# Retention in chunks of 64 on quarters of the array, with the rotation taken straight out of the banks

## The chip, the core and the metric

The kernel runs on one core of a Trainium2 chip. Its engines are TensorE (PE, matrix products; PEld is its weight load), VectorE (DVE), ScalarE (ACT), GpSimd (POOL) and SyncE (SP), which only issues transfers. Each works through its own queue in order and waits on semaphores for the others. Products land in eight banks of PSUM (128 partitions of 512 fp32 values); all other data lies in SBUF. The metric is the device time of one execution in microseconds; three runs of the kernel before took 1176.33, 1178.77 and 1178.81, median 1178.77.

## The reference

A trunk of two layers on 1024 tokens of width 1024, fp32. Layer 0 normalises the input, projects it, and runs two branches: an S5 state-space layer with a GLU, and retention with 8 heads (keys and queries of 64, values of 128). Layer 1 is a Conformer convolution module. The change is in the retention, chunk by chunk of 64 tokens:

```python
scores = jnp.einsum('bnihd,bnjhd->bnhij', qc, kc) * intra
intra_out = jnp.einsum('bnhij,bnjhe->bnihe', scores, vc)
kv = jnp.einsum('bnjhd,jh,bnjhe->bnhde', kc, k_dec, vc)
def state_step(s, kv_n):
    return chunk_decay * s + kv_n, s
cross = jnp.einsum('bnihd,ih,bnhde->bnihe', qc, q_dec, s_prev)
out = (intra_out + cross)          # then normalised per head and token
```

Queries and keys are rotated first (rope: x1 cos - x2 sin, x1 sin + x2 cos on the two halves of 32). The outcome is multiplied by a gate and goes into the output projection.

## The kernel before

The large projections run on TensorE as three fp32r products with a weight split into high and low parts (`mm3`, L276 to L278), 24 products of 512 columns for one half (512 tokens) of a 128-row tile. After layer 0's front (to 345 us) come the values (to 435), then four head pairs one after another, then the GLU and layer 1.

For one pair, `ret_proj` (L974) projects keys and queries of two heads onto 128 partitions. VectorE multiplies the bank by the token's norm factor `R` (L987), four DMAs on SyncE swap halves of 32 rows (L996), GpSimd multiplies the plain and the swapped copy by cosine and sine (L1000, L1002; two halves of 512 each), VectorE adds them (L1003). `ret_heads` (L1079) then works in blocks of 128 tokens, each two chunks with a mask that hides the second chunk from the first: it transposes the keys (L1088) and weights them with the decay (kt, L1090); makes the key-value product of each block (kv, L1107); sums the state S on VectorE (L1115, L1117), one block after another, each step needing the one before; makes the scores (sp, L1124) and masks them (sc, L1130); adds the cross product with S (L1154) and the intra product with the values (L1159) in one bank (ro) per head and half; takes mean and variance (L1168, L1169), a reciprocal root on ScalarE and VectorE (rs), and normalises (on, L1174); transposes back (rt, L1182) and multiplies by the gate (grl, L1185). Products that use half of the rows or columns of the array are written alternately so that two can run at once.

The banks are taken in turn from a small ring, so a new product can wait until an older bank was read. Pairs 0 to 2 project the keys (and then the queries) of the next pair ahead, and TensorE has these products between the retention steps. Weight lows (`weight_low`, tiles lf and lh: load, cast on ScalarE, subtraction on GpSimd or VectorE, store) for layer 1 run beside it, 18 of them by pair 2. The queues are not written out by hand: a scheduler orders the instructions of each engine by its own costs, and `issue_after` only keeps one engine's order.

## Time and profile before

| | us |
|---|---|
| median of 3 runs | 1178.77 |
| profiled execution: span of the core | 1173.9 |
| TensorE busy | 1161.3 (99%) |
| VectorE busy | 910.5 (78%) |
| GpSimd busy | 713.5 (61%) |
| ScalarE busy | 545.1 (46%) |

The span runs from the first to the last instruction; the time of a run has 4.9 us more around it. The granted clock is 0.999. In the row of a timeline stand start, length, engine, line, output and inputs, the tile of the array, shapes and a count; a bracket gives idle time and what ended it. Lengths of neighbouring products overlap, so their cost is read from one start to the next.

### The profile page before, as it was taken

To read this page: it belongs to the slowest core of one execution; us is meant where nothing else is said; L and a number is where in the kernel's file an instruction comes from. 1 tells how busy PE (TensorE), PEld (TensorE's weight loads), DVE (VectorE), ACT (ScalarE), POOL (GpSimd) and SP (SyncE) were. 2 spreads that over 40 slices of the span, in tenths; PEclk is the share of its full clock that TensorE was granted. 3 is DMA by queue.
4 is the path that set the end of the run, shared out by engine and by line. 5 is a ranking of instruction groups with operands and counts; after the bars stand their busy time and mean duration, and the time that the engine had idled before them with its cause. 6 is when DMAs were issued, how large, how long until landed. Compare 5 with 4: busy or idle time off the path is not lost.

```text
span 1173.9 us, 17492 instructions
## 1 busy us (share of the span) xinstructions
PE 1161.3 (99%) x6150; PEld 965.5 (82%) x6150; DVE 910.5 (78%) x1507; ACT 545.1 (46%) x821; POOL 713.5 (61%) x507
## 2 busy tenths in 40 slices
PE   9999999999999999999999999999999999999997
PEld 7888888888888888887788888888888888888887
DVE  7875789999717475689777888479999999999643
ACT  7212343332226642123645544367756678544662
POOL 2049999888843245664444034348894689977742
PEclk9999999999999999999999999999999999999999
DMA  9353378778789765765988468965448553357863
GB/s 344 109 178 109 134 270 312 272 269 282 273 307 325 268 228 192 251 190 180 362 313 304 160 220 268 309 232 188 161 158 306 216 182 132 134 176 243 281 247 138
DMA packets 131192, 270.66 MB, mean 231 GB/s; under 512 B 12832, under 2 KB 41760, under 8 KB 130976
## 3 DMA queue, kind: packets, MB, share of 16 engines
q1 hardware_dynamic: 129952, 265.35, 66.5%
q10 hardware_dynamic: 1152, 4.19, 0.9%
q8 instruction: 48, 0.79, 0.3%
q14 instruction: 40, 0.33, 0.1%
HBM read 193.54 MB, written 71.76 MB: 226 GB/s over the span
## 4 chain that ended last, share of the span: by engine, by line
PE 91%; DMA 4%; DVE 2%; SPq 1%; ACT 1%; POOL 1%; issue 1%; DVEq 0%; POOLq 0%; ACTq 0%
PE mm_g L277 8%; PE mm_g L278 8%; PE mm_g L276 7%; PE mm_w L278 4%; PE mm_w L277 4%; PE mm_w L276 4%; PE mm_a L278 2%; PE mm_b L277 2%; PE mm_a L276 2%; PE mm_b L278 2%; PE mm_a L277 2%; PE mm_b L276 2%; PE mm_u L278 2%; PE mm_oc L278 2%; PE mm_u L277 2%; PE mm_oc L277 2%
## 5 line engine op out<-in xcount | busy, mean ns | idle before, releaser
L1461 DVE SCALAR_TENSOR_TENSOR cv<-u,convw,cv 128x512 f32<-128x512 f32 x358 | 244.7, 750 | 5.0 <-ACT cv L1447 3.5
L1441 POOL TENSOR_TENSOR tp<-tp,tp 128x512 f32<-128x512 f32 x104 | 138.9, 1338 | 28.7 <-ACT tp L1440 23.4
L278 PE MATMUL mm_g<-xh,wl_g 128*128 128x512 f32 x256 | 100.8, 394 | 0.0
L277 PE MATMUL mm_g<-xl,wh_g 128*128 128x512 f32 x256 | 100.7, 394 | 0.0
L276 PE MATMUL mm_g<-xh,wh_g 128*128 128x512 f32 x256 | 100.5, 393 | 0.0
L1440 ACT ACTIVATE tp<-u,convw 128x512 f32<-128x512 f32 x104 | 69.6, 713 | 9.6 <-POOL tp L1441 9.4
L277 PEld LDWEIGHTS mm_g<-xl,wh_g 128*128 128x128 f32 x256 | 48.1, 188 | 11.2 <-issue 1.6
L278 PEld LDWEIGHTS mm_g<-xh,wl_g 128*128 128x128 f32 x256 | 48.0, 188 | 10.5
L276 PEld LDWEIGHTS mm_g<-xh,wh_g 128*128 128x128 f32 x256 | 48.1, 188 | 9.6
L278 PE MATMUL mm_oc<-zh,wl_woc 128*128 128x512 f32 (+1 forms) x152 | 54.5, 360 | 0.2 <-DMA wl_woc<-lo_woc 0.2
L276 PE MATMUL mm_oc<-zh,wh_woc 128*128 128x512 f32 (+1 forms) x152 | 54.3, 362 | 0.0
L277 PE MATMUL mm_oc<-zl,wh_woc 128*128 128x512 f32 (+1 forms) x152 | 54.0, 357 | 0.0
L276 PE MATMUL mm_glu<-yh,wh_glu 128*128 128x512 f32 x128 | 50.0, 392 | 1.3 <-ACT sg L1250 1.3
L277 PE MATMUL mm_u<-xl,wh_u 128*128 128x512 f32 x128 | 50.1, 391 | 1.0 <-DVE xl L390 0.9
L276 PE MATMUL mm_g<-h1h,wh_cg 128*128 128x512 f32 x128 | 50.3, 393 | 0.0
L276 PE MATMUL mm_a<-h1h,wh_ca 128*128 128x512 f32 x128 | 50.3, 393 | 0.0
L278 PE MATMUL mm_b<-h1h,wl_cb 128*128 128x512 f32 x128 | 50.3, 393 | 0.0
L232 ACT CAST lh<-lf 128x512 fp32r<-128x512 f32 x32 | 19.5, 618 | 65.9 <-DMA lf<-w_c 59.3
L278 PE MATMUL mm_a<-h1h,wl_ca 128*128 128x512 f32 x128 | 50.0, 391 | 0.0
L277 PE MATMUL mm_glu<-yl,wh_glu 128*128 128x512 f32 x128 | 50.0, 392 | 0.0
L278 PE MATMUL mm_g<-h1h,wl_cg 128*128 128x512 f32 x128 | 49.9, 390 | 0.0
L277 PE MATMUL mm_g<-h1l,wh_cg 128*128 128x512 f32 x128 | 49.9, 390 | 0.0
(811 smaller groups left out, 3637.3 us busy)
## 6 DMA issues: line engine op xcount, KB each, us to landing
wf_g<-w_ab SPq DMA_DIRECT2D x16, 512.0 KB, 5.4
a<-w_out SPq DMA_DIRECT2D x32, 256.0 KB, 4.4
ws<-a SPq DMA_DIRECT2D x32, 256.0 KB, 4.8
lf<-w_c SPq DMA_DIRECT2D x32, 256.0 KB, 5.3
wf_p<-ws SPq DMA_DIRECT2D x16, 512.0 KB, 4.1
wf_cb<-w_c SPq DMA_DIRECT2D x16, 512.0 KB, 4.9
wf_ca<-w_c SPq DMA_DIRECT2D x16, 512.0 KB, 4.7
wl_cb<-lo_cb SPq DMA_DIRECT2D x16, 512.0 KB, 3.4
```

What stands on the lines that cost most here:

```text
L232: self.nc.scalar.copy(hi[:], f[:])
L276: nc.tensor.matmul(ps, wh[:, kb, :], xh, start=start, stop=False)
L277: nc.tensor.matmul(ps, wh[:, kb, :], xl, start=False, stop=False)
L278: self.last_mm = nc.tensor.matmul(ps, wl[:, kb, :], xh, start=False, stop=stop)
L1440: nc.scalar.mul(sk[:], u[:, k:k + HALF], cw[:, nb, k:k + 1])
L1441: gp.tensor_tensor(s0[:], s0[:], sk[:], op=ALU.add)
L1461: v.scalar_tensor_tensor(dst[:], *tap, accs_[i][:], op0=ALU.mult, op1=ALU.add)
```

## The change

The retention works in chunks of 64. Each chunk's decayed keys and values make one product (15 instead of 7 states a pair), with a chunk's token half as rows and a head as columns of a quarter of the array; even and odd chunks go to two banks. Scores are 64 x 64 for each chunk and head, both heads in one bank (partitions 0 to 63 and 64 to 127), so the mask is one VectorE operation for half of the tokens instead of two. Cross and intra products are quarters too. Where a chunk's token half and the head's half differ, the intra product needs the values on the other 64 partitions: four DMAs a pair make the copy `vx` (`crossed`).

The next pair's queries are projected (`fill()`) ahead of the transposes back, and the last of the four quarters of a pair is normalised behind the first transposes. The rotation table is multiplied by `R` once, on GpSimd. Each bank of keys or queries is then read twice by VectorE (sine part, cosine part), the sine part is swapped by the four DMAs, and one addition per half on GpSimd finishes the rotation. The weight lows have three buffers instead of two and come in two groups a pair; the gate tile `grl` has two instead of three.

```diff
+        for i in range(2):
+            for c in (slice(0, HALF), slice(HALF, T)):
+                nc.gpsimd.tensor_tensor(self.rk[:, i, c], self.rk[:, i, c], self.R[:, c], op=ALU.mult)
...
-                last = nc.vector.tensor_tensor(raw[:, c], ps[:], self.R[:, c], op=ALU.mult)
+                for i in (1, 0):
+                    nc.vector.tensor_tensor(parts[nm][i][:, c], ps[:], self.rk[:, i, c], op=ALU.mult)
...
-                nc.sync.dma_start(swp[32 * b:32 * b + 32, :], raw[32 * s:32 * s + 32, :])
-            for c in cs:
-                nc.gpsimd.tensor_tensor(o[:, c], raw[:, c], tab[:, 0, c], op=ALU.mult)
-            for c in cs:
-                nc.gpsimd.tensor_tensor(swp[:, c], swp[:, c], tab[:, 1, c], op=ALU.mult)
-            return o, [lambda c=c: nc.vector.tensor_tensor(o[:, c], o[:, c], swp[:, c], op=ALU.add) for c in cs]
+                nc.sync.dma_start(swp[32 * b:32 * b + 32, :], sin[32 * s:32 * s + 32, :])
+            for c in (slice(0, HALF), slice(HALF, T)):
+                nc.gpsimd.tensor_tensor(o[:, c], cos[:, c], swp[:, c], op=ALU.add)
...
+        def value(p, c, hh, own=False):
+            d, h, b, i = p // 2, c // 8, c // 2 % 4, p % 2
+            if own and c % 2 != hh:
+                return self.vx[:, c // 2, :]
+            return vt[d][h][:, b, (2 * i + hh) * P:(2 * i + hh + 1) * P]
...
+    def crossed(self, pair):
+        d, i = pair // 2, pair % 2
+        self.vx = self.rp.tile([P, 8, P], F32, name=f"vx{pair}", tag="vx", bufs=1)
+        for h in range(2):
+            for hh in range(2):
+                to, of = slice(64 * hh, 64 * hh + 64), slice(64 - 64 * hh, 128 - 64 * hh)
+                self.nc.sync.dma_start(self.vx[to, 4 * h:4 * h + 4, :],
+                                       self.vt[d][h][of, :, (2 * i + hh) * P:(2 * i + hh + 1) * P])
...
-                    nc.tensor.matmul(ps[r, b4 * P:(b4 + 1) * P], kt[:, b, r], V(pair, b, hh),
-                                     start=True, stop=True)
+            self.chained(nc.tensor.matmul(kvs[c % 2][half(hh), col(c)], kt[half(c % 2), c // 2, half(hh)],
+                                          V(pair, c, hh)[half(c % 2)], start=True, stop=True)
+                         for c in cs for hh in range(2))
...
+            sps = self.bank(f"sp{hf}_{pair}")[:].rearrange("p (c i) -> p c i", c=8)
+            self.chained(nc.tensor.matmul(sps[half(hh), c % 8, :], K[half(hh), tok(c)], Q[half(hh), tok(c)],
                                           start=True, stop=True)
+                         for c in range(8 * hf, 8 * hf + 8) for hh in range(2))
...
+                out = lambda c, hh: pss[hh][half(c % 2), c // 2 % 4 * P:(c // 2 % 4 + 1) * P]
+                            yield nc.tensor.matmul(out(c, hh), Q[half(hh), tok(c)], S[half(hh), c - 1, :],
+                                                   start=c in (2, 1, 8, 9), stop=False)
+                        yield nc.tensor.matmul(out(c, hh), sc[half(hh), c, :], V(pair, c, hh, True)[half(hh)],
+                                               start=False, stop=c % 8 > 5)
...
+        on00, on01, on10 = (normed(*a) for a in todo[:3])
+        nxt = fill()
+        last_ro = turn(0, 1, on01, last_ro)
+        last_ro = turn(0, 0, on00, last_ro)
+        on11 = normed(*todo[3])
+        last_ro = turn(1, 0, on10, last_ro)
+        turn(1, 1, on11, last_ro)
```

How it moves instructions, at three places. First, VectorE in pair 0, from the key banks to the second mask, before:

```order
L987 TENSOR_TENSOR kraw_4259<-mm_k_0_4260,R_367 128x512
L987 TENSOR_TENSOR kraw_4259<-mm_k_1_4286,R_367 128x512
L1115 COPY S_4325<-kv_0_4326 128x128
L1117 SCALAR_TENSOR_TENSOR S_4325<-S_4325,g_3507,kv_0_4326 128x128 x3
L1117 SCALAR_TENSOR_TENSOR S_4325<-S_4325,g_3507,kv_0_4339 128x128 x2
L1130 TENSOR_TENSOR sc_0_4349<-sp_0_4351,retmask 128x512
```

and now (kv_0_4336 and kv_0_4337 hold the even and odd chunks of the first half, kv_0_4362 and kv_0_4363 those of the second):

```order
L996 TENSOR_TENSOR ksin_4247<-mm_k_1_4275,ropek 128x512
L996 TENSOR_TENSOR kcos_4246<-mm_k_1_4275,ropek 128x512
L1119 COPY S_4335<-kv_0_4336 128x128
L1121 SCALAR_TENSOR_TENSOR S_4335<-S_4335,g_3511,kv_0_4337 128x128
L1121 SCALAR_TENSOR_TENSOR S_4335<-S_4335,g_3511,kv_0_4336 128x128
...
L1121 SCALAR_TENSOR_TENSOR S_4335<-S_4335,g_3511,kv_0_4362 128x128
L1132 TENSOR_TENSOR sc_4385<-sp_0_4386,retmask 128x512
L1121 SCALAR_TENSOR_TENSOR S_4335<-S_4335,g_3511,kv_0_4363 128x128
...
L1132 TENSOR_TENSOR sc_4385<-sp_0_4404,retmask 128x512
```

The last key bank is read twice instead of once ahead of the copy; the first mask follows the ninth state and the second the fifteenth. On TensorE 11 products of the next queries stand between the two halves of the scores, where 9 stood before.

Second, VectorE in pair 3 from kt to the masks. Before (yl are splits of the GLU's input, sg a step of the GLU):

```order
L1090 TENSOR_TENSOR kt_5352<-ktp_3_5359,kdec 128x512
L1003 TENSOR_TENSOR qrot_5343<-qrot_5343,qswp_5342 128x512 x2
L1194 TENSOR_TENSOR yl_1_5620<-yf_1_5617,yh_1_5619 128x512
...
L1115 COPY S_5372<-kv_3_5373 128x128
...
L1130 TENSOR_TENSOR sc_3_5396<-sp_3_5398,retmask 128x512
L1117 SCALAR_TENSOR_TENSOR S_5372<-S_5372,g_3507,kv_3_5373 128x128
L1130 TENSOR_TENSOR sc_3_5397<-sp_3_5399,retmask 128x512
```

and now:

```order
L1101 TENSOR_TENSOR kt_5577<-ktp_3_5584,kdec 128x512
L1204 TENSOR_TENSOR yl_1_5912<-yf_1_5909,yh_1_5911 128x512
...
L1119 COPY S_5595<-kv_3_5596 128x128
L1204 TENSOR_TENSOR yl_1_5939<-yf_1_5931,yh_1_5938 128x512
L233 TENSOR_TENSOR lh_6079<-lf_6078,lh_6079 128x512
L233 TENSOR_TENSOR lh_6085<-lf_6084,lh_6085 128x512
L1121 SCALAR_TENSOR_TENSOR S_5595<-S_5595,g_3511,kv_3_5597 128x128
L1121 SCALAR_TENSOR_TENSOR S_5595<-S_5595,g_3511,kv_3_5596 128x128
```

Five splits stand between kt and the copy (three before), and one split and two weight lows between the copy and the first step; two more splits stand among the last steps. On TensorE 17 GLU products stand between the two halves of this pair's scores.

Third, TensorE behind the retention products of pair 0, now:

```order
L276 MATMUL mm_q_1_4602<-xh_1_218,wh_q_4171 128x512
L277 MATMUL mm_q_1_4602<-xl_1_219,wh_q_4171 128x512
L278 MATMUL mm_q_1_4602<-xh_1_218,wl_q_4172 128x512
L1183 MATMUL rt_1_4637<-ident,on_0_4549 128x128 x4
L1183 MATMUL rt_0_4643<-ident,on_0_4544 128x128 x4
L1183 MATMUL rt_0_4654<-ident,on_1_4554 128x128 x4
L276 MATMUL mm_k_0_4700<-xh_0_134,wh_k_4241 128x512
```

All 48 products of the next queries now come before the first transpose, 37 of them behind the retention products; 12 of the 48 came behind the first two transposes before. The last quarter's transpose (rt_1) follows 28 products of the next keys later.

More of the change, by code (lines that the diff above doesn't have):

```diff
@@ L951, in retention @@
         nc.sync.dma_start(self.reps[:], A["ret_eps"])
-        ahead = None
+        cur = list(self.ret_proj(0))[-1]
         for pair in range(4):
-            cur = list(ahead or self.ret_proj(pair))[-1]
             if pair == 0:
@@ L958, in retention, with lows @@
                 self.rp = self.pool("ret", 1, stack=st)
+                self.crossed(0)
                 ry = self.pool("retl", 1, stack=early, side="right")
-            with ExitStack() as held:
-                held.enter_context(self.tc.issue_after((self.last_rs if pair else self.last_sum).ins))
-                for k in range(LOWS * pair // 3, LOWS * (pair + 1) // 3) if pair < 3 else ():
-                    self.weight_low(ry, k, (("la", "lb"), ("la", "lb")), 2, nc.gpsimd)
+            def lows(n, behind):
+                with self.tc.issue_after(behind.ins):
+                    for k in range(n * LOWS // 6, (n + 1) * LOWS // 6) if pair < 3 else ():
+                        self.weight_low(ry, k, (("la", "lb"), ("la", "lb")), 3, nc.gpsimd)
             def turned():
+                lows(2 * pair + 1, self.last_kt)
                 if pair == 3:
@@ L968, in turned @@
                     self.lp = self.pool("l1", side="right")
+            lows(2 * pair, self.last_rs if pair else self.last_sum)
             ahead = pair in AHEAD and self.ret_proj(pair + 1)
@@ L971, in retention @@
                 next(ahead)
-            self.ret_heads(pair, *cur, V, turned)
+            cur = self.ret_heads(pair, *cur, V, turned, lambda: list(ahead)[-1] if ahead else None)
+            if pair < 3:
+                self.crossed(pair + 1)
     def ret_proj(self, pair):
         nc, A, rp = self.nc, self.A, self.r0
-        raws = {}
+        parts = {}
         def project(nm):
@@ L980, in project @@
             w = None if early else self.wnext(f"{nm}{pair}")
-            raw = raws[nm] = self.rq.tile([P, T], F32, name=f"{nm}raw_{pair}", tag="raw", bufs=2)
+            parts[nm] = tuple(self.rq.tile([P, T], F32, name=f"{nm}{part}_{pair}", tag=part, bufs=2) for part in ("cos", "sin"))
             for h in range(2):
@@ L995, in turn @@
                 s = b ^ 1
-                nc.sync.dma_start(swp[32 * b:32 * b + 32, :], raw[32 * s:32 * s + 32, :])
-            cs = [slice(h * HALF, (h + 1) * HALF) for h in range(2)]
-            for c in cs:
-                nc.gpsimd.tensor_tensor(o[:, c], raw[:, c], tab[:, 0, c], op=ALU.mult)
-            for c in cs:
-                nc.gpsimd.tensor_tensor(swp[:, c], swp[:, c], tab[:, 1, c], op=ALU.mult)
-            return o, [lambda c=c: nc.vector.tensor_tensor(o[:, c], o[:, c], swp[:, c], op=ALU.add) for c in cs]
+                nc.sync.dma_start(swp[32 * b:32 * b + 32, :], sin[32 * s:32 * s + 32, :])
+            for c in (slice(0, HALF), slice(HALF, T)):
+                nc.gpsimd.tensor_tensor(o[:, c], cos[:, c], swp[:, c], op=ALU.add)
+            return o
         project("k")
         yield None
-        krot, adds = turn("k")
-        last = project("q")
-        with self.tc.issue_after(last.ins):
-            for add in adds:
-                add()
-        qrot, qadds = turn("q")
-        if pair % 2 == 0:
-            for add in qadds:
-                add()
-            qadds = ()
-        yield krot, qrot, qadds
+        krot = turn("k")
+        project("q")
+        yield krot, turn("q")
     def ret_values(self, vp):
@@ L1122, in ret_heads @@
         for hf in range(2):
-            sps = [self.bank(f"sp{hf}{hh}_{pair}") for hh in range(2)]
-            self.chained(nc.tensor.matmul(sps[hh][:, b4 * P:(b4 + 1) * P],
-                                          K[64 * hh:64 * hh + 64, (4 * hf + b4) * P:(4 * hf + b4 + 1) * P],
-                                          Q[64 * hh:64 * hh + 64, (4 * hf + b4) * P:(4 * hf + b4 + 1) * P],
+            sps = self.bank(f"sp{hf}_{pair}")[:].rearrange("p (c i) -> p c i", c=8)
+            tok = lambda c: slice(c * 64, (c + 1) * 64)
@@ L1135, in ret_heads @@
+            self.masked[hf] = v.tensor_tensor(sc[:, 8 * hf:8 * hf + 8, :], sps,
+                                              self.mask[:, pair, :].unsqueeze(1).broadcast_to([P, 8, 64]), op=ALU.mult)
         if pair == 2:
```

128 lines of the change are left out of this document (55 added, 73 removed).

## The prediction

> **What bounds the kernel now.** I read the page's busy table first, then the chain that ended last, then the stretches of the retention stage, then the rows of TensorE there.
>
> ```profile
> PE 1161.3 (99%) x6150; PEld 965.5 (82%) x6150; DVE 910.5 (78%) x1507; ACT 545.1 (46%) x821; POOL 713.5 (61%) x507
> PE 91%; DMA 4%; DVE 2%; SPq 1%; ACT 1%; POOL 1%; issue 1%; DVEq 0%; POOLq 0%; ACTq 0%
> core 0: us, PE busy (x) PEld busy (x) DVE busy (x) ACT busy (x) POOL busy (x), PEclk, DMA share, GB/s
> 435.40:478.40 43.00, 42.73 (x277) 35.84 (x276) 24.77 (x79) 11.28 (x18) 26.10 (x18) 1.00 0.62 207
> 478.40:513.00 34.60, 34.60 (x241) 29.30 (x240) 28.21 (x76) 5.60 (x11) 24.85 (x18) 1.00 0.72 219
> 513.00:552.00 39.00, 37.96 (x255) 31.66 (x254) 32.39 (x84) 14.25 (x25) 21.28 (x14) 1.00 0.64 197
> 552.00:600.00 48.00, 45.99 (x293) 38.64 (x292) 38.48 (x97) 22.46 (x30) 19.41 (x12) 1.00 0.91 336
> 600.00:780.00 180.00, 180.00 (x802) 149.03 (x801) 130.05 (x165) 85.91 (x127) 56.95 (x39) 1.00 0.75 254
> ```
>
> TensorE sets the end: it is busy 99% of the span at full clock, and the chain of waits is 91% its own. In the four rows of the retention stage (one per head pair, roughly) it idles 0.27, 0, 1.04 and 2.01 us, while VectorE works 58 to 83% of the time and GpSimd 40 to 72%. From 600 to 780 it never idles. So a microsecond of TensorE work taken out of the retention stage should come off the end, unless a new wait replaces it. Work taken off GpSimd buys nothing by itself: nothing on the chain waits for it here.
>
> **The retention products.** The rows of TensorE around pair 0 (start, us, line, count) show what the change rewrites. An fp32 product appears as two records.
>
> ```profile
> 447.17 0.39 PE L278 MATMUL mm_k<-xh,wl_k 128*128 128x512 f32 x1
> 447.49 1.75 PE L1107 MATMUL kv<-v,kt 128*64 128x128 f32 x28
> 449.17 1.38 PE L1124 MATMUL sp<-qrot,krot 64*128 64x128 f32 x18
> 450.48 0.51 PE L276 MATMUL mm_q<-xh,wh_q 128*128 128x512 f32 x1
> 450.82 0.40 PE L277 MATMUL mm_q<-xl,wh_q 128*128 128x512 f32 x1
> ...
> 452.46 0.39 PE L278 MATMUL mm_q<-xh,wl_q 128*128 128x512 f32 x1
> 452.77 1.04 PE L1124 MATMUL sp<-qrot,krot 64*128 64x128 f32 x13
> ...
> 454.53 2.05 PE L1159 MATMUL ro<-v,sc 128*128 128x128 f32 x16
> 456.51 1.16 PE L1154 MATMUL ro<-S,qrot 64*128 64x128 f32 x16
> 457.60 2.05 PE L1159 MATMUL ro<-v,sc 128*128 128x128 f32 x16
> 459.41 0.48 PE L276 MATMUL mm_q<-xh,wh_q 128*128 128x512 f32 x1
> ```
>
> From 447.49 to 459.41 are 11.92 us, of which the nine query products in the middle take 450.48 to 452.77, 2.29. Retention proper costs 9.63 us a pair. A record of the intra product, which fills the array, costs 124 ns (16 from 454.53 to 456.51); one that fills half of it costs 60 ns in the key-value product (28 from 447.49 to 449.17), because two of them run side by side.
>
> The change cuts chunks of 128 into 64. The number of records per pair goes from 28+32+28+32=120 to 60+64+60+64=248 (15 chunks with a state and 16 with scores, two heads, two records each), each on a quarter of the array. What does a quarter cost? No row shows one. The nearest above is the half at 60 ns. The nearest below is the S5 kernel's product on four tiles of 32 columns:
>
> ```profile
> 108.80 0.45 PE L882 MATMUL kp<-Mr,s_s_cbr 128*32 128x128 f32 x8
> 109.04 0.42 PE L883 MATMUL kp<-Mi,s_s_cbi 128*32 128x128 f32 x8
> ```
>
> Eight records start within 0.24 us, 30 ns each: four tiles do run together. Row halves pair up (L1124, L1154) and column halves pair up (L1107), and the order of the new products cycles through quarters, so I take 30 ns. The scores use only two of the four quarters at a time (rows and columns of the same head) but stream 64 columns instead of 128: half the length at half the company, 30 ns again. So 248 x 0.030 = 7.4 us. Each handover between these products and the dense ones costs about 0.1 (the usual pitch is (452.46-450.82)/7 = 0.23, and 447.17 plus 0.23 is 447.40, but kv starts at 447.49; the first query product holds 0.34); four of them make 0.4. That is 7.8 against 9.63: **1.8 us saved a pair**. Bounds: at 27 ns 2.5, at 60 ns a loss of 5.6. Break-even is (9.63-0.4)/248 = 37 ns.
>
> **What may wait instead: the state chain.** The state is summed on VectorE one chunk after another, now 15 steps instead of 7.
>
> ```profile
> 447.60 0.69 DVE L987 TENSOR_TENSOR kraw<-mm_k,R 128x512 f32<-128x512 f32 x1 [4.75 <-PE mm_k L278]
> 448.63 0.29 DVE L1115 COPY S<-kv 128x128 f32<-128x128 f32 x1 [0.34 <-PE kv L1107]
> 448.96 1.95 DVE L1117 SCALAR_TENSOR_TENSOR S<-S,g,kv 128x128 f32<-128x128 f32 x5
> 450.82 0.68 DVE L1130 TENSOR_TENSOR sc<-sp,retmask 128x512 f32<-128x512 f32 x1
> 451.43 0.34 DVE L1117 SCALAR_TENSOR_TENSOR S<-S,g,kv 128x128 f32<-128x128 f32 x1
> ```
>
> A step takes 0.37 (five from 448.96 to 450.82), a mask 0.61. In front of the chain now stand two evacuations of the key bank (sine and cosine part) instead of one: 447.60+2x0.67 = 448.95, so the copy starts about 0.3 later. Then copy 0.33, eight steps 2.98, first mask 0.61 (ends 452.9), six steps 2.23 (455.1), second mask (455.7). TensorE: kv 447.5 to 449.3, first scores to 450.3, eleven query products (2.5, plus handovers) to 453.0, second scores to 454.0, first half of ro to 455.8, cross of the second half to 456.8, its intra to 457.7. What it waits for is there in time: the bank of the second ro (freed by the first mask) 1.1 us early, the last state 0.7, the second mask 1.1. So pairs 0 to 2 pay nothing, with a cover of about 0.7 us; in pairs 1 and 2 the first half of the next queries is evacuated at the same place, with the same two operations. If the cover is gone, every 0.1 us on a step costs about 1.4 us a pair, less the cover.
>
> Pair 3 is different: the listing of VectorE has five GLU splits (yl) between kt and the copy, then a sixth and two weight lows (lh), all in front of the chain, and two more inside it.
>
> ```profile
> 553.95 1.75 PE L1107 MATMUL kv<-v,kt 128*64 128x128 f32 x28 [0.67 <-DVE kt L1090]
> 554.41 1.28 DVE L1003 TENSOR_TENSOR qrot<-qrot,qswp 128x512 f32<-128x512 f32 x2
> 555.61 1.89 DVE L1194 TENSOR_TENSOR yl<-yf,yh 128x512 fp32r<-128x512 f32 x3
> 557.41 0.29 DVE L1115 COPY S<-kv 128x128 f32<-128x128 f32 x1
> 556.93 0.50 PE L277 MATMUL mm_glu<-yl,wh_glu 128*128 128x512 f32 x1
> 563.73 1.04 PE L1124 MATMUL sp<-qrot,krot 64*128 64x128 f32 x13
> 568.56 2.05 PE L1159 MATMUL ro<-v,sc 128*128 128x128 f32 x16
> ```
>
> At 0.6 a split: kt 0.6 more, splits 3.1, copy 0.3, split and two lows 1.9, seven steps 2.6, mask 0.6, seven steps and two splits 3.8: the last state is there 12.9 us after kv started. TensorE has kv, two score halves, 17 GLU products (3.9) and half of ro, about 10, before it needs that; the second cross and intra then end near 14.7. Before, the same block ended at 568.56+1.81 = 570.4, 16.4 after kv's start, with more GLU products in it: 556.93 to 563.73 are 6.8 us, 29 or 30 of them. The 12 or so that now come behind the block are 2.8 us. So pair 3 gets 14.7+2.8-16.4 = **1.1 us slower**, instead of 1.8 faster. Bounds: 1.8 gained if the lows come late enough not to matter, 3 lost if the first low waits for its load.
>
> **Next queries in front of the transposes.** The idle time of TensorE that this can take away (total, times, longest):
>
> ```profile
> PE rt L1182 <- DVE on L1174: 1.0, 1, 1.0
> ```
>
> 37 products (8.4 us) now cover the normalisation of the first three quarters in pair 0; I count **1.0** gained, the bounds being 0 and this. The fourth quarter is normalised after 28 further products or, later, after 4; VectorE's rows put it about 1.3 ahead.
>
> **Rotation.** Removed: GpSimd's products (four of eight operations a pair) and VectorE's additions; added: two VectorE products a bank instead of one, and once four products of the table on GpSimd. All of it costs nothing while TensorE's projections cover it, 48 products of 0.23 (11 us) between a projection and its use. At the start the cover is thin:
>
> ```profile
> 355.33 2.53 POOL L1000 TENSOR_TENSOR krot<-kraw,ropek 128x512 f32<-128x512 f32 x2 [18.34 <-DMA ropek<-rope_k]
> 353.29 0.39 PE L1062 MATMUL mm_v<-wh_V,xh 128*128 128x512 f32 x1
> ```
>
> The table lands at 355.3, four products of 1.27 make it ready at 359.1 (first sine half) to 360.4, and the first key bank is free at 360.5. The second half of the queries needs that bank; it now comes after 49 value products, 353.3 + 49 x 0.23 = 364.6. About 4 us to spare; a table that lands 5 us later would cost 1. The swaps on SyncE:
>
> ```profile
> 475.51 2.80 SPq L996 DMA_DIRECT2D qswp<-qraw  x4
> 483.52 3.91 DVE L1003 TENSOR_TENSOR qrot<-qrot,qswp 128x512 f32<-128x512 f32 x2
> 489.18 1.38 PE L1124 MATMUL sp<-qrot,krot 64*128 64x128 f32 x18
> ```
>
> The queries of pair 1 were swapped from 475.5, added up at 483.52+3.91 = 487.4 and used at 489.2. Their swap still queues on SyncE behind weight-low stores, and on GpSimd behind twelve casts of 1.3 instead of ten, but the third buffer lets the loads go earlier and the last step is two additions of 1.27 on GpSimd. I count nothing; without that cover each microsecond that the swap is late is one of TensorE's. Four DMAs a pair copy crossed values on SyncE; they need only the values, which are done before pair 0.
>
> **Sum.** Pairs 0 to 2: -5.4; pair 3: +1.1; transposes: -1.0; total -5.3. The profiled execution had 1173.9 of span, 4.9 under the median of 1178.77 (1176.33 to 1178.81); 1168.6 + 4.9 = **1173.5**.
>
> **Rivals.**
> *Quarters only pair up* (the slower side): 60 ns as for halves. 248 x 0.060 + 0.4 = 15.3, +5.6 a pair, +22 in all, 1200. It decides from 37 ns on. For it: no row has both row and column tiles. Against: the kp rows. 0.10.
> *The chain is late everywhere*: steps of 0.5 rather than 0.37 (held up by other work on VectorE's memory), 14 x 0.13 = 1.8 us a pair, less the cover of 0.7 in three of them: +5.1 in all, 1178.6, no change. For it: one and the same addition of L1003 lasts 1.95 us at 483.52 and 0.64 at 554.41. Against: the steps themselves never varied by more than 12 ns (shortest, median, longest below). 0.17.
>
> ```profile
> L1117 DVE SCALAR_TENSOR_TENSOR S<-S,g,kv x24: 336/347/348, 449.0 to 565.4; 128x128 f32<-128x128 f32 x24
> ```
>
> *Two heads' scores take turns at one bank*: both heads now write one bank, where each had its own. 64 x 0.030 more, 1.9 a pair, 7.7 in all, less the 1.1 of pair 3, which it would cover: 1180, no change. 0.08. [...] No run so far shows it.
> *The turned queries of pair 1 come late*: SyncE's queue holds the swap behind a store whose cast waits for its load. From the additions' end to the use are 1.8 us, and two additions of 1.27 in place of 2.53+3.91 leave about 4 more; beyond 6 us late each microsecond counts. Held by 15 us, sp waits 9: 1182.5. For it: the swap of 475.51 already stood behind such stores. Against: the third buffer. 0.07.
> *All covers hold, pair 3 too, at 27 ns*: 1167. 0.08.
> The forecast keeps 0.50. A measurement here tells no change from 0.2%, 2.4 us. Faster is the forecast, the last rival and a little of the second, 0.60; within 0.2% most of the second and of the third, 0.20; slower the first, the fourth and the rest of those two, 0.20. The range reaches from the best case to the late queries: 1167 to 1183.
>
> **What would show it.** Right: ro records starting 27 to 32 ns apart; no TensorE wait for S or sc in pairs 0 to 2; a wait of 1 to 3 us for S in pair 3; the start of pair 1's kv about 2 us earlier than 487.5. Wrong: records 50 ns apart, a wait of sp for qrot or of mm_q for kcos, or scores at twice the cost of the cross product.

## The result and the profile after

The changed kernel took **1187.03 us** (median of 4 runs, 1186.53 to 1189.67) against 1177.87 (4 runs, 1176.33 to 1178.81) for the kernel before: ratio 1.0078, 95% interval 1.0064 to 1.0092, **9.2 us slower**. The forecast was 1173.5 with a range to 1183.

The two profiles lie 14.0 us apart (spans of 1187.9 and 1173.9). In the recorded runs of the kernel before a time is 1.7 to 1.9 us longer than its span, not 4.9 (that figure sets the median against the span of one faster execution); by that before's execution was an estimated 2.2 under its median, and after's was its slowest run, 2.6 over. So the stages below show where time goes, and some five microseconds of their differences belong to this pair of executions. The first fence is the stretches of the kernel before, the second those of the changed kernel, cut at the first product of each stage: the values, the four pairs with the GLU, the output product, the convolution. Columns: the stretch, its length, then busy time of each engine with its count, and the granted clock after the engines.

```profile
353.30:435.60 82.30, 82.30 (x361) 67.60 (x360) 51.56 (x58) 50.09 (x55) 25.73 (x14) 1.00 0.80 268
435.60:643.30 207.70, 204.39 (x1250) 171.19 (x1249) 154.80 (x376) 74.82 (x117) 111.85 (x70) 1.00 0.76 258
643.30:765.90 122.60, 122.60 (x548) 101.49 (x547) 92.24 (x113) 56.74 (x83) 35.34 (x27) 1.00 0.73 243
765.90:1132.90 367.00, 366.63 (x1637) 301.83 (x1636) 327.91 (x492) 231.44 (x348) 280.10 (x205) 1.00 0.58 197
```

```profile
353.70:440.60 86.90, 84.03 (x362) 68.70 (x361) 50.87 (x58) 50.16 (x55) 26.85 (x14) 0.98 0.77 255
440.60:650.40 209.80, 199.46 (x1762) 166.36 (x1761) 151.46 (x398) 69.63 (x111) 89.54 (x57) 0.98 0.82 263
650.40:777.00 126.60, 123.47 (x549) 101.21 (x548) 92.95 (x116) 59.11 (x87) 36.93 (x27) 1.00 0.70 229
777.00:1147.00 370.00, 366.93 (x1638) 301.82 (x1636) 327.77 (x492) 231.72 (x348) 280.13 (x205) 1.00 0.59 199
```

Read the second row of each. TensorE's busy time in the pairs fell from 204.39 to 199.46 us, as intended. But its idle time there (length less busy) rose from 3.3 to 10.3, so the stretch grew by 2.1. The value stage grew by 4.6, the output product by 4.0 and the convolution by 3.0, though the change does not touch their arithmetic. What TensorE waited for, from the waits of the changed kernel (total, times, longest), and behind them the longest of the kernel before:

```profile
PE mm_glu L276 <- ACT sg L1260: 4.1, 2, 2.8
PE mm_v L1058 <- DVE v L1036: 2.9, 1, 2.9
PE rt L1183 <- DVE mv L1168: 2.8, 1, 2.8
PE mm_w L278 <- DVE wl_p L167: 2.2, 2, 1.4
PE sp L1129 <- DVE S L1121: 2.0, 1, 2.0
PE mm_a L278 <- DMA wl_ca<-lo_ca: 1.6, 1, 1.6
```

```profile
PE mm_glu L276 <- ACT sg L1250: 1.3, 1, 1.3
```

**The clock.** The granted clock is the share of its full clock that TensorE is given. About five of the 9.2 us are lost by work at half clock. In the stretches above the granted clock never fell in the kernel before. In the changed kernel it fell to half three times, for 3.41 us each: once in the value stage behind the wait for v, and twice in the pairs, behind the waits for mv and for S. TensorE's rows, each time the 3.41 us ahead of a fall and then the fall (busy time behind the length, then the granted clock):

```profile
392.02:395.43 3.41, 0.65 (x3) 1.00 1.02 383
395.43:398.84 3.41, 3.41 (x10) 0.50 0.82 282
542.20:545.61 3.41, 1.06 (x8) 1.00 0.69 165
545.62:549.03 3.41, 2.95 (x7) 0.50 0.67 148
562.68:566.09 3.41, 1.45 (x42) 1.00 1.06 407
566.10:569.51 3.41, 3.41 (x65) 0.50 1.06 408
```

At a granted clock of 0.50, with dense products 0.43 us apart instead of 0.23 (value stage), I count half of the busy time in such a stretch as lost: 1.7 us in the value stage, where it makes up the 4.6 together with the wait of 2.9, and (2.95 + 3.41) / 2 = 3.2 us in the pairs. So I estimate TensorE's work in the pairs at full clock at 199.46 - 3.2 = 196.3 us: the change saved 8.1 us there, and 7.0 us more of idle time and 3.2 us of half clock turned that into a loss of 2.1. It is not this one execution: the clocks of the four runs are 0.994 to 0.995, and 1 less the clock, times the span, is 6.8 us in their mean; in the 102 runs of the kernel before that stand beside the experiments it is 1.8.

**The retention products themselves are what was hoped for.** TensorE in pair 0 of the changed kernel:

```profile
452.40 1.86 PE L1113 MATMUL kv<-v,kt 64*64 64x128 f32 x58
454.20 1.09 PE L1129 MATMUL sp<-qrot,krot 64*64 64x64 f32 x30
455.22 0.50 PE L276 MATMUL mm_q<-xh,wh_q 128*128 128x512 f32 x1
...
457.94 0.97 PE L1129 MATMUL sp<-qrot,krot 64*64 64x64 f32 x26
458.92 0.86 PE L1154 MATMUL ro<-S,qrot 64*64 64x128 f32 x23
...
462.52 0.50 PE L278 MATMUL mm_q<-xh,wl_q 128*128 128x512 f32 x1
```

A group's time runs from its first start to its last end, so with 0.27 for one record of ro the 23 start (0.86 - 0.27) / 22 = 27 ns apart, kv's 58 28 ns, and the scores, at 0.22 for one, 30 ns. Retention takes 455.22 - 452.40 plus 462.52 - 457.94, 7.4 us against 9.63. There is no wait in it.

**The value stage.** SyncE's queue before (first fence) and after (second): a row of several transfers lasts until the last of them could be issued.

```profile
356.69 1.07 SPq L1029 DMA_DIRECT2D xf<-xt  x2
357.80 1.06 SPq L931 DMA_DIRECT2D yp<-y_d  x2
359.68 4.32 SPq L1029 DMA_DIRECT2D xf<-xt  x4
```

```profile
350.20 2.55 SPq L1025 DMA_DIRECT2D xf<-xt  x4
352.85 14.82 SPq L931 DMA_DIRECT2D yp<-y_d  x4
...
371.69 0.99 SPq L1025 DMA_DIRECT2D xf<-xt  x1
375.35 0.37 SPq L931 DMA_DIRECT2D yp<-y_d  x1
375.85 2.07 SPq L1025 DMA_DIRECT2D xf<-xt  x2
```

Four loads of the pass over y now stand in a row. They have two buffers (bufs=2), so the third waits until ScalarE has used the first, and the queue stands for 14.8 us. The second group of value loads (xf) is issued from 371.7 and not from 359.7, one by one and again with yp between them. The values' splits, the evacuation v and TensorE follow late (TensorE's rows):

```profile
394.78 0.47 PE L1058 MATMUL mm_v<-wh_V,xth 128*128 128x512 f32 x1 [2.87 <-DVE v L1036]
395.64 0.63 PE L1058 MATMUL mm_v<-wh_V,xth 128*128 128x512 f32 x1
396.07 0.63 PE L1059 MATMUL mm_v<-wl_V,xth 128*128 128x512 f32 x1
```

Not all of this delay comes from yp: in run 5, which takes yp off this queue, the group still begins at 371.7. There it goes out in a row, and ScalarE casts the last of it (xth) at 381.68 instead of 386.75. The late beginning may come from the table (argued, not tested): VectorE's first product out of the banks waits for it until 359.98, where VectorE began at 352.81 before, and the first cast of xf comes at 369.3 instead of 357.6.

**Pairs 2 and 3.** VectorE's rows, first of the kernel before in pair 2, then of the changed kernel in pair 2 and in pair 3:

```profile
529.55 5.74 DVE L1194 TENSOR_TENSOR yl<-yf,yh 128x512 fp32r<-128x512 f32 x4
```

```profile
530.10 0.68 DVE L1132 TENSOR_TENSOR sc<-sp,retmask 128x512 f32<-128x512 f32 x1
530.70 5.87 DVE L1204 TENSOR_TENSOR yl<-yf,yh 128x512 fp32r<-128x512 f32 x6
536.50 1.67 DVE L1167 BATCH_NORM_STATS2 st<-ro 128x6 f32<-128x128 f32 x8
...
556.53 4.16 DVE L1204 TENSOR_TENSOR yl<-yf,yh 128x512 fp32r<-128x512 f32 x5
560.62 0.28 DVE L1119 COPY S<-kv 128x128 f32<-128x128 f32 x1
560.82 0.68 DVE L1204 TENSOR_TENSOR yl<-yf,yh 128x512 fp32r<-128x512 f32 x1
561.42 1.28 DVE L233 TENSOR_TENSOR lh<-lf,lh 128x512 fp32r<-128x512 f32 x2
562.63 2.63 DVE L1121 SCALAR_TENSOR_TENSOR S<-S,g,kv 128x128 f32<-128x128 f32 x7
```

In pair 2 six low halves of the GLU's input (yl) take 5.87 us between the second mask and the statistics; the transposes wait 2.8 for the statistics (mv). The low halves are not new there: before, four of them took 5.74 at the same place. Counted from the start of the pair's kv (522.08 before, 522.61 now), the statistics begin at 13.9 us instead of 13.1, and the transposes even at 21.9 instead of 22.8. But TensorE is done with all that stands ahead of the transposes at 19.1 instead of 21.7: the quarters save 2.2, and two fewer products the rest. So what was saved there became a wait for VectorE. In pair 3 six low halves and two weight lows (lh) stand in front of the chain, and the scores wait 2.0 for S. Behind them the GLU waits 2.8 for a gate (sg) on ScalarE's queue, where the cast of a weight low had waited 5.2 for its load.

### The profile page after: what moved, and what is told of

The parts are those of the page before. It is cut to its first block, busy times and chain, and to the rows that moved or that the text cites. A ratio compares the mean times of both kernels' runs of the same rounds, so it can differ in the third digit from the quotient of the medians.

```text
span 1187.9 us, 18547 instructions
## 1 busy us (share of the span) xinstructions
PE 1159.5 (98%) x6662; PEld 962.4 (81%) x6662; DVE 906.0 (76%) x1531; ACT 542.8 (46%) x819; POOL 693.9 (58%) x495
## 4 chain that ended last, share of the span: by engine, by line
PE 82%; DMA 9%; DVE 4%; ACT 1%; POOL 1%; issue 1%; SPq 1%; DVEq 0%; POOLq 0%; ACTq 0%
PE mm_g L277 7%; PE mm_g L278 7%; PE mm_g L276 7%; PE mm_w L278 3%; PE mm_w L276 3%; PE mm_w L277 3%; PE mm_a L278 2%; PE mm_b L277 2%; PE mm_a L277 2%; PE mm_a L276 2%; PE mm_b L278 2%; PE mm_oc L278 2%; PE mm_u L278 2%; PE mm_b L276 2%; PE mm_u L277 2%; PE mm_oc L277 2%
## 5 line engine op out<-in xcount | busy, mean ns | idle before, releaser
L278 PE MATMUL mm_glu<-yh,wl_glu 128*128 128x512 f32 x128 | 50.5, 394 | 0.0
```

Of the source, the lines that this page charges most:

```text
L278: self.last_mm = nc.tensor.matmul(ps, wl[:, kb, :], xh, start=False, stop=stop)
```

## The experiments

The theories in the expectations. **A**: the quarters save what was planned, and the losses come from queues that the change set in another order (in the value stage above all). **B**: the state chain, twice as long, overloads VectorE. **C**: the queries in front of the transposes do harm. Later ones are defined in the expectations where they first appear. All ratios are to the kernel before, measured beside each run (medians of 1176.9 to 1178.4), with their 95% interval; times of different runs are compared by these ratios; a diff is against the changed kernel unless it says otherwise.

**1. The chunks alone.** The changed kernel with the rotation of before (one product out of the bank, table products on GpSimd, additions on VectorE):

```diff
-                for i in (1, 0):
-                    nc.vector.tensor_tensor(parts[nm][i][:, c], ps[:], self.rk[:, i, c], op=ALU.mult)
+                last = nc.vector.tensor_tensor(raw[:, c], ps[:], self.R[:, c], op=ALU.mult)
...
+        with self.tc.issue_after(self.last_kt.ins):
+            for add in qadds:
+                add()
```

> The changed kernel with the old rotation (raw product, swap, two GpSimd products and one VectorE addition per half); chunks of 64, next queries ahead of the transposes, three buffers of weight lows kept. Theory A (the quarters save 2.2 to 2.7 us a pair as planned, and the loss comes from queues that were put in another order around it, the first of them, 4.6 us in the value stage, by the new rotation): keys of pair 0 transposed at 435 to 437 instead of 440.5, pairs 0 and 1 each 2 us or more shorter than before, total 1176 to 1183. Theory B (the chunks themselves cost the time, since VectorE's longer state chain pushes everything behind it): the value stage may be in time, but the total stays at 1184 to 1188.

Measured 1191.1 us, ratio 1.0118 (1.0101 to 1.0136). The value stage is in time again (82.7 us), which A predicted, but the pairs with the GLU take 223.7 us in place of 209.8, which it did not: TensorE's waits there are headed by

```profile
PE rt L1195 <- DVE on L1189: 7.3, 1, 7.3
PE ro L1166 <- DVE S L1133: 4.8, 1, 4.8
PE rt L1195 <- DVE mv L1180: 4.0, 1, 4.0
```

The time lies outside both ranges. The waits are of B's kind: VectorE's queue is late for S and for the normalisation. That the rotation's additions on it make it late is argued and not shown; in pair 3 VectorE itself stood 2.95 us for GpSimd (yg) and 1.39 for ScalarE (yh) between the steps of the chain. With the chunks, the rotation out of the banks is worth nearly 5 us (1.0118 against 1.0078).

**2. The rotation alone.** The kernel before with the new rotation (diff against it, the reverse of the one above):

```diff
-                last = nc.vector.tensor_tensor(raw[:, c], ps[:], self.R[:, c], op=ALU.mult)
+                for i in (1, 0):
+                    nc.vector.tensor_tensor(parts[nm][i][:, c], ps[:], self.rk[:, i, c], op=ALU.mult)
```

> The kernel before with the new rotation alone (table times R on GpSimd, two VectorE products a bank, one GpSimd addition per half); chunks of 128 and all else as before. Theory A: the value stage loses about 4.6 us, the pairs stay as they were, total 1179 to 1184. Theory B: no loss in the value stage or one made up later, total 1176 to 1179.

Measured 1182.1, ratio 1.0046 (1.0030 to 1.0063). SyncE's queue shows the same row (four yp from 353.2 on, 14.7 us), the wait for v 4.0, the value stage 88.8 us against 82.3, and the pairs 207.0, no worse than before. A holds for the value stage: the loss comes with the rotation, without any chunk of 64.

**3. The next queries at their old place**, behind the transposes:

```diff
-            cur = self.ret_heads(pair, *cur, V, turned, lambda: list(ahead)[-1] if ahead else None)
+            cur = list(ahead or self.ret_proj(pair))[-1]
+            self.ret_heads(pair, *cur, V, turned, lambda: None)
```

> The changed kernel with the next pair's queries taken up behind the transposes, as the kernel before has it. Theory A: the place of the queries is not a cause; waits of the transposes come back (0.5 to 2 us), the total is 1185 to 1191. Theory C (the wait of 2.8 us for the normalised values in pair 2 and what follows come from queries in front of the transposes): that wait and its 1 us of slow clock go, total 1180 to 1184.

Measured 1193.5, ratio 1.0136 (1.0121 to 1.0151). So the queries in front are worth 0.0058 x 1177, nearly 7 us, though the two intervals allow 4 to 9, and C falls: without them `rt` waits 3.1 for `on` and 1.9 for `mv`, and the granted clock is 0.98 from 345 to 435.4 us, 0.96 from there to 478.4 and 0.93 from 552 to 600, by an estimate four stretches of 3.41 us at half clock instead of three.

**4. The loads of yp behind the value loads**, still on SyncE:

```diff
+        with self.tc.issue_after(self.last_fetch.ins):
+            nc.sync.dma_start(yt[:], self.y_d[cb].rearrange("i h g m -> (h g) i m"))
```

> The changed kernel; only the loads of the GELU passes in the value stage (yp) are issued on SyncE behind the last of the value loads instead of four in a row ahead of them. Theory A: the 2.9 us wait of the value products at 394.8 and the slow clock behind it go (4.6 us), keys of pair 0 transposed at 436, and this stays to the end: 1181 to 1184. Theory B: the stage is in time, but the gain is lost before the end: 1185 to 1188.

Measured 1186.9, ratio 1.0088 (1.0067 to 1.0108): nothing gained. The value loads went out in a row (367.6), but now ScalarE stood before a late yp, with the casts of the next values behind it:

```profile
390.11 2.02 ACT L934 ACTIVATE yn<-yp 128x1024 f32<-128x1024 f32 x1 [5.26 <-DMA yp<-y_d]
```

The wait of mm_v for v was 3.1. The place on SyncE was changed, and the same pair of queues still met; by itself this run does not tell A from a late VectorE.

**5. The loads of yp on ScalarE's queue**, which itself frees their buffers:

```diff
-        nc.sync.dma_start(yt[:], self.y_d[cb].rearrange("i h g m -> (h g) i m"))
+        nc.scalar.dma_start(yt[:], self.y_d[cb].rearrange("i h g m -> (h g) i m"))
```

> The changed kernel, but the loads yp of the pass over y are issued on ScalarE's queue (the engine that frees their buffers itself), so that none stands in front of the value loads on SyncE. Theory A (the value stage is late because the value loads queue behind yp): value loads issued by 362, the wait for v at 394.8 gone, the value stage ends within 1.5 us of before's time, total 1180 to 1184. Rival F (the two products per half on VectorE make its own value splits late, whatever the loads do): wait of 2 us or more for v stays, total 1185 to 1188.

Measured 1183.2, ratio 1.0043 (1.0027 to 1.0059). The stretch of the values:

```profile
353.40:435.60 82.20, 82.20 (x362) 67.64 (x361) 48.06 (x58) 48.83 (x54) 26.08 (x14) 1.00 0.83 270
```

TensorE never idles there. One detail of the expectation was wrong: the second group of loads still went out at 371.7, but all four in a row; that sufficed. With run 2 this shows the value stage's loss and its cause, the loads of yp on SyncE.

**6. The GLU's low halves on GpSimd**, all sixteen, behind pair 3's key and query additions:

```diff
-                self.split(f, a, b, v, None if halves else self.masked_2 if h == 0 else self.last_kt if kb < 6 else self.masked[0])
+                self.split(f, a, b, v if halves else gp, None if halves else self.adds["k"] if h == 0 else self.adds["q"])
```

> The changed kernel, but the 16 low halves of the GLU's input (yl) are formed on GpSimd in place of VectorE: the first eight behind the key addition of pair 3, the others behind its query addition. Theory D (VectorE is overfull in pairs 2 and 3 because the state chain, the splits and the lows share its one queue): the 2.8 us wait of the transposes in pair 2 falls under 1.2, the 2.0 us wait for S in pair 3 under 0.8, the GLU stage begins 3 to 6 us earlier, total 1180 to 1184; the 4.9 us of the value stage stay. Rival E (what binds there are the transfers on SyncE's queue and ScalarE's order, VectorE only looks late): waits stay within 1 us of what they were, total 1185 to 1189.

Measured 1184.0, ratio 1.0043 (1.0028 to 1.0057). The wait of `rt` in pair 2 (2.8) is gone and one of 0.9 stands in pair 3; that of `sp` for S fell from 2.0 to 0.2, with 0.6 for S and 1.7 for the mask `sc` behind it; and the pairs with the GLU took 206.0 us in place of 209.8. Another new wait came, 4.2 us of the GLU products for GpSimd's `yl`. D (VectorE overfull there) is shown, at a gain of 3 to 4 us.

**7. Both edits.**

> Both edits together (yp on ScalarE's queue, the GLU's low halves on GpSimd). A and D: the gains add, 1174 to 1179, no slower than the kernel before. Rival G (what is gained is given back at the next load or cast, since the stages behind are bound by the weights' arrival): 1181 to 1186.

Measured 1178.1, ratio 1.0002 (0.9988 to 1.0016): the gains add, and the changed kernel is level with the one before. The two causes carry the whole loss of 0.8%. It is not faster, though TensorE has less to do; the stretch of the pairs with the GLU:

```profile
436.10:643.50 207.40, 201.04 (x1761) 166.92 (x1760) 145.16 (x383) 71.89 (x114) 109.02 (x73) 0.98 0.85 268
```

It still idles 6.4 us in the pairs, 4.6 of them for `yl`, and 9.6 us of its busy time there (548.50 to 555.32 and 568.98 to 572.39) passed at half clock, with products 0.43 us apart in both (551.42 to 551.85, 571.66 to 572.09). At full clock I estimate the work at 201.04 - 4.8 = 196.2 us. So it saves 8.2 us against the kernel before, and 3.1 more of idle time and 4.8 of half clock use that up.

**8. The swaps on GpSimd's queue as well.**

```diff
-                nc.sync.dma_start(swp[32 * b:32 * b + 32, :], sin[32 * s:32 * s + 32, :])
+                nc.gpsimd.dma_start(swp[32 * b:32 * b + 32, :], sin[32 * s:32 * s + 32, :])
```

> The kernel with both edits, and besides the rotation's four swapping transfers a turn on GpSimd's queue in place of SyncE's. If the swaps, which wait for the sine product, also hold the loads behind them on SyncE (theory A in its wider form): 1 to 3 us faster than with both edits alone. If only yp did: within 1.5 us of it, or slower, since GpSimd now stands waiting for the sine products in front of its own low halves.

Measured 1178.8, ratio 1.0021 (1.0001 to 1.0041), no gain over run 7. In its profile the pairs are the shortest of the changed forms so far, and the output product gives it back:

```profile
435.90:639.90 204.00, 198.70 (x1762) 165.35 (x1761) 144.14 (x381) 69.96 (x111) 120.60 (x97) 0.99 0.84 270
639.90:765.60 125.70, 123.20 (x548) 101.28 (x547) 92.98 (x117) 59.13 (x86) 35.86 (x27) 1.00 0.73 237
```

**9. The low halves shared between GpSimd and VectorE**, with yp on ScalarE's queue, and **10.** the same with gates and weight lows held behind the last masked score:

```diff
+                self.split(f, a, b, v if halves or h and kb < 4 else gp, None if halves else self.adds["k"] if h == 0 else self.last_kt if kb < 4 else self.adds["q"])
...
+            with self.tc.issue_after(self.masked[1].ins):
+                v.scalar_tensor_tensor(sg[:], sg[:], 1.0, yg[:], op0=ALU.add, op1=ALU.mult)
```

> yp on ScalarE's queue, and the GLU input's low halves shared out: the eight of the first half and the last four of the second on GpSimd, the first four of the second half on VectorE behind the key transposes of pair 3 (where it stood idle for 11.8 us with all sixteen on GpSimd). Theory D: the 4.0 us wait of the GLU products for GpSimd's yl shrinks under 2, and the time falls 1 to 4 us under that of all sixteen on GpSimd: 1173 to 1177, faster than the kernel before. Rival G (the stage behind is bound by transfers on SyncE, a wait only moves): 1177 to 1180.

> The same, and the GLU's gate products and weight lows on VectorE are held behind the second masked score of pair 3, so that nothing stands inside the state chain. Theory B in its narrow form (what is queued between the chain's steps in pair 3 costs time): the 1.7 us wait for sc in pair 3 falls under 0.6 and the time falls another 1 to 2 us, 1172 to 1176. Rival: the lows come later, their transfers with them, and the wait turns up at the GLU's gates or at the next weights, no change or up to 3 us slower.

Measured 1181.4, ratio 1.0030 (1.0018 to 1.0042), and 1180.9, ratio 1.0021 (1.0010 to 1.0032). Run 9 missed both of its ranges; run 10 missed theory B's, and its rival (no change, waits further on) had it. In run 9 the wait for `yl` fell to 1.9 as expected, and the transposes of pair 3 waited 7.6 us for `on`. In run 10 that wait was 4.6, and others came at the output product (3.1 for wl_p, 1.9 for the last gates sg).

Theory G (a wait taken away turns up at the next place) fits both runs.

**11. The same edits in the kernel before** (yp on ScalarE's queue, the low halves but four on GpSimd):

> The kernel before, with the same two kinds of edit (yp on ScalarE's queue; the GLU input's low halves on GpSimd but for four). If these edits repair only what the change disturbed (theories A and D): 1175 to 1180, the kernel before has nothing to gain from them, and the repaired change is faster than it by 1 to 5 us. If they remove a weakness that both kernels have: 1170 to 1174, and the change itself stays worth nothing.

Measured 1176.9, ratio 0.9992 (0.9983 to 1.0001), no change that can be told. Its pairs are shorter than those of the kernel before, its output product longer:

```profile
436.30:640.90 204.60, 204.25 (x1250) 171.10 (x1249) 148.06 (x363) 71.61 (x114) 122.92 (x81) 1.00 0.79 261
640.90:765.80 124.90, 123.21 (x549) 101.31 (x548) 91.13 (x114) 57.16 (x85) 39.95 (x27) 1.00 0.70 233
```

This kernel waits 0.35 us in the pairs, and still 2.3 of the 3.1 us it gained there are gone by the convolution. So the stage behind takes back most of the gain in the kernel before too.

**12 to 15. Fewer weight lows in the GLU stage.** In the changed kernel ScalarE waits 29.7 us there for the loads of the 14 weight lows, before 18.7 (ScalarE's waits between 545 and 645, of before, then of after):

```profile
ACT lh L232 <- DMA lf<-w_c: 18.7, 9, 3.5
```

```profile
ACT lh L232 <- DMA lf<-w_c: 29.7, 9, 9.5
```

Eight lows are left there when the pairs take 24. The edit is made in the changed kernel, in run 7's, in run 10's and in run 11's:

```diff
-LOWS = 18
+LOWS = 24
```

> The changed kernel with 24 of the 32 weight lows in the retention's pairs in place of 18, so that 8 and not 14 are left in the GLU stage; nothing else. Theory H (in the GLU stage the lows have one buffer each of two; their loads' waits, 29.7 us in all on ScalarE's queue, hold the gates behind them and eat what the pairs gained): the stage up to the weights of the output product (mm_w) begins 3 to 6 us earlier, total 1179 to 1184. Rival: the lows added to the pairs disturb GpSimd's and SyncE's queues there as much, total 1185 to 1190.

> yp on ScalarE's queue, all sixteen GLU lows yl on GpSimd, and 24 weight lows in the pairs. Theory H: 2 to 5 us under the same without the third edit (1178.1): 1173 to 1176. Rival (yl waits for GpSimd or the weights wl_p set the end of the stage): 1177 to 1181.

> The kernel with the state chain first (1180.9, 11.8 us ahead of the kernel before at pair 3's transposes, all of it lost by the output product) and 24 weight lows in the pairs. Theory H: it loses less than half of that: 1172 to 1176. Rival as above: 1178 to 1182.

> The kernel before with yp on ScalarE's queue, the GLU's low halves on GpSimd but for four (1176.9) and 24 weight lows in the pairs. If the lows bind the GLU stage whatever the retention does (theory H in its wide form): 1172 to 1175, and the change's own worth is what the repaired changed kernel is under it. If the lows bind only the changed kernel: 1176 to 1178.

Measured 1186.7, ratio 1.0076 (1.0054 to 1.0098); 1182.6, 1.0046 (1.0028 to 1.0064); 1183.0, 1.0041 (1.0027 to 1.0055); 1179.8, 1.0016 (1.0004 to 1.0028). H missed four times, and only run 12 came where its rival had it. In run 12 ScalarE's wait fell to 16.8 and the output product no longer waited for wl_p (its stretch 124.2 us in place of 126.6); in run 14 that wait fell from 3.1 to 0.5, so the lows do make it; but the pairs with the GLU grew from 209.8 to 213.7, with a new wait of 2.8 for `on`. Six more lows cost as much in the pairs as they free behind, or more, in the kernel before too (0.9992 to 1.0016).

**16 to 18. The output product's first four weight lows on GpSimd**, in run 8's kernel; then two low halves ahead of the query addition as well; and the first of these in run 11's kernel:

```diff
-        return self.wload_split(self.wload_f32(src, name), name, self.nc.vector)
+        return self.wload_split(self.wload_f32(src, name), name, self.nc.gpsimd if i == 1 else self.nc.vector)
```

> The kernel with yp on ScalarE's queue, yl and the swaps on GpSimd (1178.8; 204.0 us from pair 0's key transposes to the output product, against 207.7 before and 209.8 changed), and besides the low halves of the output product's first four weights (wl_p, which stand behind the splits of t2 and the yr0g additions in VectorE's order) on GpSimd. Theory I (what the pairs gain is given back because wl_p comes in its old place in VectorE's order): its two waits of 2.1 and 1.2 us go, total 1174 to 1177. Rival: the next late thing takes them over (the conv's lows from memory, wl_ca), 1178 to 1180.

> The same, and the first two low halves yl of the second half ahead of pair 3's query addition on GpSimd. The products of the second half then find them: the 2.4 us wait for yl in pair 3 falls under 1, total 1 to 3 us under the run before it. Rival: the query addition comes later by as much and the scores wait for it, no change.

> The kernel before, with yp on ScalarE's queue, its yl (but four) and those four weight lows wl_p on GpSimd. Theory I holds for it too (its own pairs gained 3 us by the first two edits and lost 2.3 at the output product): 1173 to 1176. If it gains as much as the changed kernel does, the change is worth less than 2 us once both queues are in order; if it stays at 1176 to 1178 the difference is what the change is worth.

Measured 1184.0, ratio 1.0049 (1.0030 to 1.0068); 1187.5, 1.0085 (1.0065 to 1.0105); 1182.0, 1.0035 (1.0023 to 1.0047). All three are slower than either side expected. Theory I falls: the product still waits 2.2 for wl_p (2.5 in run 8), now for GpSimd's, and 3.9 for ScalarE's `m` behind. GpSimd in run 16:

```profile
647.01 5.60 POOL L167 TENSOR_TENSOR wl_p<-wf_p,wh_p 128x1024 fp32r<-128x1024 f32 x2
```

One of these low halves takes 2.4 to 2.8 us there and 1.2 on VectorE (run 8), so that the products wait for it about as long as before. In run 17 the wait for yl fell from 3.5 to 2.7 us only, and `ro` in pair 3 waited 4.9 for S: its rival came true, and worse.

**What stays open.** The two causes of the loss are settled: with both undone the changed kernel is level with the one before. Where the 8 us of work that TensorE saves in the pairs go is settled for run 7, in which idle time and half clock use them up there. Behind the pairs it is settled only in part: waits at the GLU, at the output product and at the convolution's weights take their turn, each moved by an edit and none removed for good. Which load or cast is the last of that row was not found, no run was made to see with shorter waits of TensorE whether the clock stays at full, and no form of either kernel beat the kernel before by more than a measurement tells.

## Why the prediction was wrong, and where it was right

**Quarters (-1.8 a pair): right, a little small.** Records of 27 to 30 ns, 7.4 us a pair against 9.63, so -2.2; the 8.1 us estimated for the four pairs at full clock agree. The rival in which quarters only pair up is out. So is the one in which the heads' scores take turns at one bank: its price was 60 ns a record, the row of 30 above has 30 ns; the two heads write different halves of the bank's partitions.

**State chain in pairs 0 to 2 (nothing): right for the chain, wrong for what is queued behind it.** A step takes 348 ns in the changed kernel, and no score or cross product waits for S there; so the rival of slower steps is out. So is that of the late queries: no product waits for qrot. But in pair 2 the transposes waited 2.8 us where 1.0 had stood: TensorE was there 2.65 us sooner, and VectorE, with the low halves behind the second mask and then the statistics, only 0.9. The prediction looked for the wait at S and did not follow VectorE's queue past the second mask.

**Pair 3 (+1.1): the place was right, the term too small.** The wait for S is 2.0, within the 1 to 3 given. The term left out what follows: 1.7 us of half clock behind that wait, and the gates sg, for which the GLU waits 4.1 in place of 1.3. Run 6 took most of S's wait away, and that of the transposes in pair 2, and was worth 3 to 4 us.

**Queries in front of the transposes (-1.0): right in sign, far too small.** Run 3 puts it near 7 us. The term was read off the wait of the kernel before; with a longer chain that wait would have grown, and the edit also covers that.

**Rotation (nothing): the step that failed.** "All of it costs nothing while TensorE's projections cover it" was worked out for the table, the swaps and the key bank, and TensorE waited for none of these in the value stage. The table reached VectorE at 359.98, 359.1 in the forecast. But alone the rotation costs 5.4 us (0.0046 x 1177, run 2), because the new order on SyncE puts four loads with two buffers in front of the value loads; with these on ScalarE's queue (run 5) the value stage is in time. I had compared the swaps' neighbours on that queue, not every load that changed its place. In the other direction run 1 shows a worth that I had not counted: without the rotation's edit the chunks cost 1.2%.

**A wait priced at its length: the term that is missing everywhere.** The prediction counts a microsecond of waiting as a microsecond. Behind three of the waits (2.87 for v, 2.8 for mv, 2.0 for S) the granted clock was 0.50 for 3.41 us each, by my estimate 1.7, 1.5 and 1.7 us more, about 5 of the 9.2 in all. No term of the sum, no rival and no bound has this.

**"A microsecond of TensorE work taken out of the retention stage should come off the end, unless a new wait replaces it": the new waits came, and not where it looked.** It rested on TensorE never idling from 600 to 780. TensorE was just met there by weights and gates that came in time and not early; run 11 gained 3.1 us in the pairs and kept 0.8 until the convolution. And in pair 2 it was VectorE that set when the transposes could start, so that time taken from TensorE ahead of them came back as a wait.

Of the marks named in advance, the records and the wait for S came as told. Pair 1's kv began at 490.2, not 2 us before 487.5: it had started 4.9 late and made up 2.2.

## What to carry to other kernels

When an edit changes which tiles exist, list every queue's order for the whole stage and look for loads of a ring of n buffers that now stand n + 1 deep: everything behind them waits for whoever frees the ring (14.8 us here), and issuing them on that engine's own queue mended it here (run 5). Follow a longer chain past its last step to what stands behind it on the same engine. And a stretch in which TensorE never idles shows only that its inputs came in time, not how early: look at the margin of the next weights before counting a gain upstream as a gain at the end. Price a new wait of TensorE with the half clock that can follow it: here the waits of 2.87 (v), 2.8 (mv) and 2.0 us (S) were each followed by one stretch of 3.41 us, worth up to 1.7 us by estimate, and one of 2.8 for sg was not.

## What the hardware did that was not expected

After the wait of 2.87 us in the value stage eight products started 0.43 us apart (395.64, 396.07 above) instead of 0.23, so the wait cost 1.7 us more than its length; the granted clock of those 3.41 us is 0.50. After the wait of 3.1 us in run 4 the products ran at the full pace, 0.23 to 0.24 us apart (395.24 to 395.95), and the granted clock from 345 to 435.4 us is 1.00. The times at which the falls start show a pattern. In the profile of the changed kernel the clock falls at 395.43, 545.62 and 566.10 us, 44 and then 6 times 3.413 us apart, and again at 1183.91, behind TensorE's last product, 181 times 3.413 later: as if frames of that length ran on beside the program. That is read from these four times alone. In the frames ahead of the first three falls TensorE idled 2.76, 2.35 and 1.96 us. The end of a frame split the wait of 2.8 for sg, 1.34 and 1.47, and no fall followed. Between 60 and 1165 us every other frame of this profile, counted from the same falls, has at most 1.63 us of idle time (777.72 to 781.13), and none was followed by half clock. In the profile of the kernel before no 3.41 us of that stretch hold more than 1.33 us of idle time (the wait of 1.3 for sg), and the clock never fell there. How much idle time goes ahead of a fall was not tested by an edit.
